# Giving out 48 late modulation blocks anew, and cutting the up projection's first parts into 18, 9 and 7 pairs

## The chip, the cores and the metric

The kernel runs on one core of a Trainium2 chip. The metric is the device time of one execution, in microseconds (us). Before the change three runs gave 1270.31, 1273.58 and 1273.60 us, a median of 1273.58 us. A further execution was recorded by the hardware profiler. Engines carry the names of the profile: PE is the matrix engine, DVE the vector engine, ACT the scalar engine, POOL the general engine, and SP the engine whose queue issues the loads.

## The reference

One decoder layer over 256 tokens of width 2048, in float32. A conditioning vector c gives six modulation vectors through `silu(c) @ w_ada + b_ada` (2048 by 6 x 2048): shift and gain of the mixer's norm, a gate g1, shift and gain of the ffn's norm, and a gate g2.

```python
h   = modulate(rms_norm(x, norm_mix), mix_shift, mix_gain)
x   = x + g1 * (concat(retention(h), rwkv7(h), moba(h)) @ w_out)   # all three from h @ w_in
h   = modulate(rms_norm(x, norm_ffn), ffn_shift, ffn_gain)
u,v = split(depthwise_conv3(h @ w_up))                             # 2 x 5632 columns
x   = x + g2 * ((silu(v) * u) @ w_down)
out = rms_norm(x, norm_final)
```

This is a sketch of it: the RWKV-7 branch ends with a norm over each head and a gate, and each row of the formula reads the modulation vectors that stand in it.

## The kernel before, in words

**Weights as one stream.** All activations are held with the features on the partitions, in 16 blocks of 128 features by 256 tokens. Each weight matrix is cut into 128 by 128 blocks, 3200 in all, in the order in which PE uses them (`weight_order`). One load brings 16 blocks (1 MB): 52 loads for the input projection ("in"), 16 for the output projection ("out"), 88 for "up" and 44 for "down". Half a load, 8 blocks, is called a chunk here: in has the chunks 0 to 103, out 104 to 135, up 136 to 311, down 312 to 399.

**Three matmuls for a block.** For precision each chunk is split in two halves by `convert_until`: ACT casts it (`hi`, L465), then DVE subtracts (`lo`, L466). PE then runs three matmuls for each block: hi by hi (L1226), hi by the low half of the activations (L1227), and lo by hi (L1228), so a chunk is 24 matmuls. `hi` and `lo` have three buffers each (`CONVB`), so the split of chunk c can only start when PE is through with chunk c-3, and without its `lo` PE stops within the first block of chunk c.

**Modulation blocks in the same stream.** The 96 rows of `w_ada` (1 MB each) are loaded in the same stream. DVE multiplies each by silu(c) and sums it in one instruction (L420, in `ada_block`), and one small instruction adds the bias (L428) or makes the gain of the norm of it (L422). `LATE_ADA` says how many of the 48 blocks of g1, ffn shift and ffn gain go to each part of the stream, spread evenly within it: first the tail of the input projection (19 loads, chunks 66 to 103), then four groups of five out loads (the last has one), then the first three parts of up.

**Raw tiles.** Loaded blocks lie in three raw tiles of 1 MB (`RAWB`), in which modulation blocks and early weights take turns. From chunk 116 on, weights are loaded as two halves into tiles of another pool (`LEAD` limits how many; L347 issues every load). SP issues loads in order, and a load waits there until its tile is free.

**Out.** In the out stage the RWKV branch is still being finished in short tasks between the chunks (`run_tasks`): a state's pieces sp (L921), sb (L976), u (L948), U (L953), the sums yps (L984), then a head norm whose root is found by Newton steps of small DVE rows (`rsqrt`, L240 to L245), the result yc (L1002), its transpose yt on PE (L1006), the mixing rows (L1011, L1013) and the split of them (`mxhi` L435, `mxlo` L436). The outputs of out are added to x with L1066, and at the start of out x comes by four loads, each behind a small copy that reads one element of g1 (L1055, `out_start`).

**Up.** `ffn_start` waits for the sum of squares of the last out tile (acc, L1080), takes the mean on PE (nps, L1084), finds the root by the same Newton steps (DVE) and spreads it on PE (rs, L390). The first four blocks of features (`EARLY` tiles, `ffn_early`) are worked before the root is known and scaled afterwards (L1120). Then DVE makes the normed activations, rows xn (L446) and hlo (L448), one pair for each block of features. `UP_BEGUN` says how many of the 44 pairs of up columns are begun with features 0 to 3, 0 to 7 and 0 to 11 only.

**What sets the order.** The order of the source is handed to a scheduler, which may move instructions on each engine; what stands in the program of an engine then runs from top to bottom.

Of the kernel before, what the change touches and what calls it, by code (L numbers as in the profile page):

```python
# [17 lines left out]
NF = 16  # L18
# [11 lines left out]

VISITS = (30, 20, 17)

UP_BEGUN = (22, 8, 4)


def spread(*lists):
# [5 lines left out]
def weight_order():  # L42
# [51 lines left out]
    n = 0  # L94
    for b in UP_BEGUN:
        pairs.append(list(range(n, n + b)))
# [62 lines left out]
ADA = {"mix_shift": 0, "mix_gain": 16, "g1": 32, "ffn_shift": 48, "ffn_gain": 64, "g2": 80}  # L159
RAWB, EXTRA, CONVB, AHEAD = 3, 2, 3, 2  # L160

LATE_ADA = (18, 3, 3, 2, 0, 7, 7, 8)

EARLY = 8

# [2 lines left out]

CONST_PAD, SMALL_PAD = 32, 16

LEAD = ((116, 0), (145, 8), (152, 6), (164, 4), (172, 3), (186, 1))


def trunk(tc, A):
    nc = tc.nc
    V, S, PE, G = nc.vector, nc.scalar, nc.tensor, nc.gpsimd
# [27 lines left out]
    def s4(name, dt=F32):  # L204
        return arena.tile([128, 4, T], dt, tag="s4", name=nm(name))
# [98 lines left out]
    parts += [(up[cut_up[g]:cut_up[g + 1]], 2) for g in range(3)]  # L304
    for n, (part, after) in zip(LATE_ADA, parts):
        n_part = len(part) - after
# [12 lines left out]
    def lead():  # L319

        c = len(chunks)
        return next((n for end, n in LEAD if c < end), 0)

# [88 lines left out]
    mod = {n: const.tile([128, NF], F32, name=f"mod_{n}") for n in ADA}  # L412
# [635 lines left out]
    def run_until(ready):  # L1048
        while not ready():
            run_tasks(1)  # L1050

    def out_start():
        for g in range(4):
            x = s4("x1")
            S.copy(x[:, 0, 0:1], mod["g1"][:, NF - 1:])  # L1055
            G.dma_start(x, A["xT"][:, 4 * g:4 * g + 4, :])
            x1.append(x)
        for g in (0, 2):
            run_until(lambda: g in finished)
# [132 lines left out]
    first_down = first_up + len(ORDER["up"]) // 8  # L1192
    hooks.setdefault(first_mix, []).append(lambda: new_stage(mixer, "mixer", bufs=1))
    hooks.setdefault(first_out, []).append(out_start)
    hooks.setdefault(first_out + WAITS[0], []).append(lambda: wait_for(3))
    hooks.setdefault(first_out + WAITS[1], []).append(lambda: wait_for(1))
# [117 lines left out]
```

## Time and profile before

| what | value |
|---|---|
| median of three runs | 1273.58 us |
| profiled execution, whole | 1276.42 us |
| its span (first to last instruction) | 1274.6 us |
| mean granted clock of PE | 0.987 of full |
| PE busy | 1227.2 us (96%) |
| DVE busy | 1030.1 us (81%) |
| ACT busy | 651.2 us (51%) |
| data moved | 320.58 MB, 252 GB/s mean |

Busy shares are averages over the whole span. A stage is read better by itself: where PE is busy for the whole of a stretch, only less work for PE would shorten it; where PE has gaps, the row on PE's waits names the engine that ended each. In a timeline row the first number is the start, the second the time until the result is there. The next row of the same engine often starts a little earlier than the sum of the two, so the distance between two starts is what an instruction costs its engine.

### The profile page before, as it was taken

To read this page: it belongs to the slowest core of one execution; us is meant where nothing else is said; L and a number is where in the kernel's file an instruction comes from. 1 tells how busy PE (TensorE), PEld (TensorE's weight loads), DVE (VectorE), ACT (ScalarE), POOL (GpSimd) and SP (SyncE) were. 2 spreads that over 40 slices of the span, in tenths; PEclk is the share of its full clock that TensorE was granted. 3 is DMA by queue.
4 is the path that set the end of the run, shared out by engine and by line. 5 is a ranking of instruction groups with operands and counts; after the bars stand their busy time and mean duration, and the time that the engine had idled before them with its cause. 6 is when DMAs were issued, how large, how long until landed. Compare 5 with 4: busy or idle time off the path is not lost.

```text
span 1274.6 us, 25479 instructions
## 1 busy us (share of the span) xinstructions
PE 1227.2 (96%) x10608; PEld 1205.3 (95%) x10608; DVE 1030.1 (81%) x1607; ACT 651.2 (51%) x1043; POOL 42.6 (3%) x41
## 2 busy tenths in 40 slices
PE   5899999999999999899999999999999999999995
PEld 4899999989998889899999999999999999999995
DVE  6988989989988589899887999899866766666444
ACT  4354443756434534566555666666555544444441
POOL 0000000000000000600000000000000000000000
PEclk7999999999999999999999999999999999999998
DMA  9899877876654569677984565565655677767551
GB/s 387 343 365 334 341 300 273 300 261 229 230 179 166 199 240 412 241 281 254 357 308 172 193 223 200 197 232 198 216 196 188 228 263 271 285 250 288 196 199 67
DMA packets 49940, 320.58 MB, mean 252 GB/s; under 512 B 5536, under 2 KB 6048, under 8 KB 15776
## 3 DMA queue, kind: packets, MB, share of 16 engines
q1 hardware_dynamic: 48528, 315.10, 67.5%
q0 software_dynamic: 1008, 3.67, 0.8%
q8 instruction: 83, 1.36, 0.4%
q14 instruction: 33, 0.27, 0.1%
q10 hardware_dynamic: 288, 0.17, 0.1%
HBM read 316.83 MB, written 2.10 MB: 250 GB/s over the span
## 4 chain that ended last, share of the span: by engine, by line
PE 83%; DVE 7%; issue 5%; ACT 2%; DMA 1%; POOL 1%; DVEq 0%; ACTq 0%; POOLq 0%
PE mm L1226 25%; PE mm L1227 24%; PE mm L1228 24%; DVE raw L420 3%; DVE lo L466 2%; ACT hi L465 1%; PE pair L1228 1%; PE xx L787 1%; PE pair L1227 1%; PE pair L1226 1%; POOL acc L1080 1%; DMA dec<-dec 1%; PE akv L800 1%; DMA x<-xT 1%; PE cb L406 0%
## 5 line engine op out<-in xcount | busy, mean ns | idle before, releaser
L466 DVE TENSOR_TENSOR lo<-raw,hi 128x1024 fp32r<-128x1024 f32 x400 | 489.1, 1225 | 164.5 <-ACT hi L465 161.5
L465 ACT CAST hi<-raw 128x1024 fp32r<-128x1024 f32 x400 | 419.0, 1049 | 387.3 <-PE mm L1227 335.1
L1226 PE MATMUL mm<-hhi,hi 128*128 128x256 f32 x2016 | 561.0, 278 | 0.5 <-DVE proj L501 0.5
L1228 PE MATMUL mm<-hhi,lo 128*128 128x256 f32 x2016 | 559.8, 278 | 1.1 <-DVE lo L466 1.1
L1227 PE MATMUL mm<-hlo,hi 128*128 128x256 f32 x2016 | 559.8, 278 | 0.0
L1228 PEld LDWEIGHTS mm<-hhi,lo 128*128 128x128 f32 x2016 | 378.9, 188 | 2.4 <-DVE lo L466 1.9
L1226 PEld LDWEIGHTS mm<-hhi,hi 128*128 128x128 f32 x2016 | 379.4, 188 | 1.4 <-DVE proj L501 0.7
L1227 PEld LDWEIGHTS mm<-hlo,hi 128*128 128x128 f32 x2016 | 378.9, 188 | 0.9 <-issue 0.2
L420 DVE SCALAR_TENSOR_TENSOR raw<-raw,cb 128x2048 f32<-128x2048 f32 x96 | 219.8, 2290 | 6.1 <-DMA raw<-w_ada 4.9
L1226 PE MATMUL mm<-ghi,hi 128*128 128x256 f32 x704 | 194.8, 277 | 0.0
L1227 PE MATMUL mm<-glo,hi 128*128 128x256 f32 x704 | 194.8, 277 | 0.0
L1228 PE MATMUL mm<-ghi,lo 128*128 128x256 f32 x704 | 194.8, 277 | 0.0
L1226 PEld LDWEIGHTS mm<-ghi,hi 128*128 128x128 f32 x704 | 132.2, 188 | 0.0
L1228 PEld LDWEIGHTS mm<-ghi,lo 128*128 128x128 f32 x704 | 132.2, 188 | 0.0
L1227 PEld LDWEIGHTS mm<-glo,hi 128*128 128x128 f32 x704 | 132.1, 188 | 0.0
L1226 PE MATMUL mm<-mxhi,hi 128*128 128x256 f32 x256 | 72.9, 285 | 2.4 <-DVE x L1066 2.4
L1227 PE MATMUL mm<-mxlo,hi 128*128 128x256 f32 x256 | 73.1, 286 | 0.0
L1228 PE MATMUL mm<-mxhi,lo 128*128 128x256 f32 x256 | 72.5, 283 | 0.0
L1080 POOL TENSOR_TENSOR acc<-acc,nsq 128x256 f32<-128x256 f32 x28 | 36.6, 1309 | 792.9 <-ACT nsq L1079 792.5
L1226 PEld LDWEIGHTS mm<-mxhi,hi 128*128 128x128 f32 x256 | 49.0, 191 | 3.4 <-DVE x L1066 2.6
L1226 PE MATMUL pair<-hhi,hi 128*128 128x256 f32 x160 | 45.1, 295 | 6.9 <-ACT hi L465 5.0
L1228 PEld LDWEIGHTS mm<-mxhi,lo 128*128 128x128 f32 x256 | 48.8, 191 | 1.4 <-DVE lo L466 0.7
(292 smaller groups left out, 1281.8 us busy)
## 6 DMA issues: line engine op xcount, KB each, us to landing
raw<-w_ada SPq DMA_DIRECT2D x96, 1024.0 KB, 5.1
raw<-w_up SPq DMA_DIRECT2D x67, 1024.0 KB, 4.8
raw<-w_in SPq DMA_DIRECT2D x52, 1024.0 KB, 6.1
raw<-w_down SPq DMA_DIRECT2D x44, 1024.0 KB, 4.9
raw<-w_up SPq DMA_DIRECT2D x42, 512.0 KB, 8.4
raw<-w_out SPq DMA_DIRECT2D x18, 512.0 KB, 9.9
raw<-w_out SPq DMA_DIRECT2D x7, 1024.0 KB, 4.8
x<-xT SPq DMA_DIRECT2D x4, 512.0 KB, 5.6
```

The source lines that it names most:

```text
L420: V.scalar_tensor_tensor(raw, raw, 1.0, cb, op0=OP.mult, op1=OP.mult, accum_out=m)
L465: S.copy(flat(hi), src)
L466: V.tensor_tensor(flat(lo), src, flat(hi).bitcast(F32), op=OP.subtract)
L787: return PE.matmul(pe[e][:, o:o + 128], (Bt, Kt)[i][pb, f, sl], (At, Rt)[n][pb, f, sl], start=True, stop=True)
L800: PE.matmul(ps[:, 128 * i + 64 * e:128 * i + 64 * e + 64], xv[:, e, 128 * i:128 * i + 128], vT[:, h, 64 * hd:64 * hd + 64], start=True, st ...
L1080: (V if t == NF - 1 else G).tensor_tensor(norm["acc"], norm["acc"], sq, op=OP.add)
L1226: PE.matmul(ps, whi[:, j], hi, start=first and not (two and t % 2), stop=False, skip_group_check=two)
L1227: PE.matmul(ps, whi[:, j], lo, start=False, stop=False, skip_group_check=two)
L1228: PE.matmul(ps, wlo[:, j], hi, start=False, stop=last, skip_group_check=two)
```

## The change

Three tables of numbers and one index are changed.

```diff
-UP_BEGUN = (22, 8, 4)
+UP_BEGUN = (18, 9, 7)
-LATE_ADA = (18, 3, 3, 2, 0, 7, 7, 8)
+LATE_ADA = (8, 7, 5, 4, 0, 8, 8, 8)
-LEAD = ((116, 0), (145, 8), (152, 6), (164, 4), (172, 3), (186, 1))
+LEAD = ((116, 0), (145, 8), (152, 6), (164, 4), (172, 3), (188, 1))
     def out_start():
         for g in range(4):
             x = s4("x1")
-            S.copy(x[:, 0, 0:1], mod["g1"][:, NF - 1:])
+            S.copy(x[:, 0, 0:1], mod["g1"][:, 7:8])
             G.dma_start(x, A["xT"][:, 4 * g:4 * g + 4, :])
```

Of the 48 late blocks, 8 instead of 18 are spread over the tail of the input projection, 16 instead of 8 over out, 24 instead of 22 over the first three parts of up. The small copy ahead of the loads of x now reads element 7 of g1, the last that the input projection's tail still makes. The first three parts of up, 34 pairs together in both, have 11, 8 and 6 loads before, with limits at chunks 158, 174 and 186, and end at chunks 154, 172 and 193 after.

The scheduler answers with another order on every engine. Three places are shown. The first is SP, the loads just ahead of the first out load that goes in halves (out load 7 of 16, chunks 118 and 119). Before:

```order
L347 DMA raw_5201<-w_out 128x2048
L347 DMA raw_5315<-w_out 128x2048
L347 DMA raw_5391<-w_ada 128x2048
L347 DMA raw_5449<-w_ada 128x2048
L347 DMA raw_5441<-w_out 128x1024
L347 DMA raw_5442<-w_out 128x1024
```

After:

```order
L347 DMA raw_5367<-w_out 128x2048
L347 DMA raw_5417<-w_ada 128x2048
L347 DMA raw_5451<-w_ada 128x2048
L347 DMA raw_5490<-w_ada 128x2048
L347 DMA raw_5523<-w_ada 128x2048
L347 DMA raw_5594<-w_ada 128x2048
L347 DMA raw_5661<-w_ada 128x2048
L347 DMA raw_5419<-w_out 128x1024
L347 DMA raw_5420<-w_out 128x1024
```

Two modulation loads stood ahead of that weight load, and now six stand there.

The second place is DVE at the same chunks. The first row is the `lo` of chunk 117, the last that of chunk 118. Before:

```order
L466 TENSOR_TENSOR lo_5511<-raw_5315,hi_5510 128x1024
L976 TENSOR_TENSOR sb_4905<-sp_5233,pcs_5262 64x4x64 x2
L422 SCALAR_TENSOR_TENSOR mod_ffn_gain<-mod_ffn_gain,bias_166,vec 128x1
L420 SCALAR_TENSOR_TENSOR raw_5449,mod_ffn_shift<-raw_5449,cb 128x2048
L953 TENSOR_TENSOR U<-u_5286,R_3478 32x512
L466 TENSOR_TENSOR lo_5566<-raw_5441,hi_5565 128x1024
```

After, the first twelve rows from the `lo` of chunk 117 on:

```order
L466 TENSOR_TENSOR lo_5487<-raw_5367,hi_5486 128x1024
L245 SCALAR_TENSOR_TENSOR rsy_5127<-rsa_5128,rsy_5127 128x8
L420 SCALAR_TENSOR_TENSOR raw_5417,mod_ffn_shift<-raw_5417,cb 128x2048
L243 SCALAR_TENSOR_TENSOR rsa_5128<-rsy_5127 128x8
L1066 SCALAR_TENSOR_TENSOR x_4710<-mm_5496,mod_g_162,x_4710 128x256
L244 TENSOR_TENSOR rsa_5128<-rsa_5128,var_5124 128x8
L428 TENSOR_TENSOR mod_ffn_shift<-mod_ffn_shift,vec 128x1
L420 SCALAR_TENSOR_TENSOR raw_5451,mod_ffn_gain<-raw_5451,cb 128x2048
L245 SCALAR_TENSOR_TENSOR rsy_5127<-rsa_5128,rsy_5127 128x8
L422 SCALAR_TENSOR_TENSOR mod_ffn_gain<-mod_ffn_gain,bias_166,vec 128x1
L1002 TENSOR_TENSOR yc_5088<-yc_5088,rsy_5127 128x512
L420 SCALAR_TENSOR_TENSOR raw_5490,mod_ffn_shift<-raw_5490,cb 128x2048
```

Then come four pairs of mixing rows (L1011, L1013), eight instructions, and after them, up to the `lo` of chunk 118:

```order
L953 TENSOR_TENSOR U<-u_5160,R_3458 32x512
L1066 SCALAR_TENSOR_TENSOR x_4710<-mm_5549,mod_g_162,x_4710 128x256
L436 TENSOR_TENSOR mxlo_5155<-mix_rwkv_4873,mxhi_5154 128x4x128
L428 TENSOR_TENSOR mod_ffn_shift<-mod_ffn_shift,vec 128x1
L420 SCALAR_TENSOR_TENSOR raw_5523,mod_ffn_gain<-raw_5523,cb 128x2048
L976 TENSOR_TENSOR sb_4870<-sp_5054,pcs_5166 64x4x64 x2
L422 SCALAR_TENSOR_TENSOR mod_ffn_gain<-mod_ffn_gain,bias_166,vec 128x1
L420 SCALAR_TENSOR_TENSOR raw_5594,mod_ffn_shift<-raw_5594,cb 128x2048
L953 TENSOR_TENSOR U<-u_5224,R_3458 32x512
L466 TENSOR_TENSOR lo_5534<-raw_5419,hi_5533 128x1024
```

Between two `lo` that stood one L420 apart, five L420 stand now, with the end of a head norm and its mixing rows.

The third place is DVE early in up, between the `lo` of chunk 143 and that of chunk 144. Before, from the `lo` of chunk 142 to that of chunk 144:

```order
L466 TENSOR_TENSOR lo_6477<-raw_5959,hi_6476 128x1024
L448 SCALAR_TENSOR_TENSOR hlo_6380<-xn_6424,mod_ffn_shift,hhi_6379 128x256
L448 SCALAR_TENSOR_TENSOR hlo_6380<-xn_6428,mod_ffn_shift,hhi_6379 128x256
L446 SCALAR_TENSOR_TENSOR xn_6466<-x_4743,mod_ffn_gain,rs_ffn 128x256
L446 SCALAR_TENSOR_TENSOR xn_6480<-x_4743,mod_ffn_gain,rs_ffn 128x256
L466 TENSOR_TENSOR lo_6516<-raw_5960,hi_6515 128x1024
L448 SCALAR_TENSOR_TENSOR hlo_6465<-xn_6466,mod_ffn_shift,hhi_6464 128x256
L448 SCALAR_TENSOR_TENSOR hlo_6465<-xn_6480,mod_ffn_shift,hhi_6464 128x256
L466 TENSOR_TENSOR lo_6558<-raw_6099,hi_6557 128x1024
```

After, twelve rows that begin three rows behind the `lo` of chunk 143; the row of L245 is the last Newton step of the ffn norm, which stood behind the `lo` of chunk 140 before:

```order
L420 SCALAR_TENSOR_TENSOR raw_6620,mod_ffn_gain<-raw_6620,cb 128x2048
L245 SCALAR_TENSOR_TENSOR rsy_6276<-rsa_6277,rsy_6276 128x2
L420 SCALAR_TENSOR_TENSOR raw_6705,mod_ffn_shift<-raw_6705,cb 128x2048
L446 SCALAR_TENSOR_TENSOR xn_6363<-x_4707,mod_ffn_gain,rs_ffn 128x256
L446 SCALAR_TENSOR_TENSOR xn_6379<-x_4704,mod_ffn_gain,rs_ffn 128x256
L1120 TENSOR_TENSOR up_6320<-up_6320,rs_ffn 128x1024
L448 SCALAR_TENSOR_TENSOR hlo_6362<-xn_6363,mod_ffn_shift,hhi_6361 128x256
L422 SCALAR_TENSOR_TENSOR mod_ffn_gain<-mod_ffn_gain,bias_166,vec 128x1
L446 SCALAR_TENSOR_TENSOR xn_6383<-x_4704,mod_ffn_gain,rs_ffn 128x256
L428 TENSOR_TENSOR mod_ffn_shift<-mod_ffn_shift,vec 128x1
L420 SCALAR_TENSOR_TENSOR raw_6778,mod_ffn_gain<-raw_6778,cb 128x2048
L420 SCALAR_TENSOR_TENSOR raw_6790,mod_ffn_shift<-raw_6790,cb 128x2048
```

Ten more rows follow (four L448, four L446, one L1120, one L422) before the `lo` of chunk 144. Where two L448 stood between the two `lo`, four L420, seven L446, five L448 and two L1120 stand now.

## Rows read from the trace of the kernel before

**Rows 1.** Stretches: start:end, length; PE, PEld, DVE, ACT, POOL busy (count), PEclk, DMA, GB/s.
```profile
203.90:441.00 237.10, 228.17 (x1874) 212.87 (x1873) 209.73 (x444) 127.89 (x277) 5.75 (x9) 0.99 0.63 227
418.20:421.60 3.40, 3.40 (x15) 3.04 (x14) 1.16 (x1) 1.33 (x3) 0.00 (x0) 0.50 0.92 316
541.50:561.90 20.40, 20.34 (x169) 20.16 (x169) 20.11 (x38) 13.53 (x39) 0.00 (x0) 1.00 0.76 287
600.00:700.00 100.00, 100.00 (x885) 100.00 (x884) 81.40 (x104) 53.97 (x79) 0.00 (x0) 1.00 0.78 281
```

**Rows 2.** PE's waits from 203.9 us on: total us, times, longest us.
```profile
PE mo_pt L605 <- ACT mo_p L602: 2.7, 2, 2.3
...
PE y L874 <- DVE bd L864: 1.4, 1, 1.4
```

**Rows 3.** Timeline of DVE in out: start, us, engine, line, operation.
```profile
456.84 0.69 DVE L1002 TENSOR_TENSOR yc<-yc,rsy 128x512 f32<-128x512 f32 x1
457.44 2.28 DVE L420 SCALAR_TENSOR_TENSOR raw<-raw,cb 128x2048 f32<-128x2048 f32 x1
...
459.65 0.60 DVE L1011 SCALAR_TENSOR_TENSOR mix_rwkv<-yt,vec,rwm 128x128 f32<-128x128 f32 x2
...
461.74 0.67 DVE L953 TENSOR_TENSOR U<-u,R 32x512 f32<-32x512 f32 x1
462.34 1.20 DVE L466 TENSOR_TENSOR lo<-raw,hi 128x1024 fp32r<-128x1024 f32 x1
463.48 0.67 DVE L436 TENSOR_TENSOR mxlo<-mix_rwkv,mxhi 128x512 fp32r<-128x512 f32 x1
464.08 0.86 DVE L976 TENSOR_TENSOR sb<-sp,pcs 64x256 f32<-64x256 f32 x2
464.97 0.48 DVE L1066 SCALAR_TENSOR_TENSOR x<-mm,mod_g,x 128x256 f32<-128x256 f32 x1
465.37 1.22 DVE L466 TENSOR_TENSOR lo<-raw,hi 128x1024 fp32r<-128x1024 f32 x1
```

**Rows 4.** The same timeline, the `lo` of chunks 117 and 118.
```profile
467.74 1.22 DVE L466 TENSOR_TENSOR lo<-raw,hi 128x1024 fp32r<-128x1024 f32 x1
...
472.93 1.23 DVE L466 TENSOR_TENSOR lo<-raw,hi 128x1024 fp32r<-128x1024 f32 x1
```

**Rows 5.** Pieces of the chain that ended last, in out: start, us, what.
```profile
457.58 0.66 PE yt L1006 x4
458.24 0.99 PE u L948 x8
...
463.19 0.62 PE sp L921 x32
```

**Rows 6.** Timeline of ACT in out.
```profile
420.27 0.37 ACT L435 CAST mxhi<-mo_o 128x256 fp32r<-128x256 f32 x1 [0.59 <-PE mo_o L615]
...
496.40 1.05 ACT L465 CAST hi<-raw 128x1024 fp32r<-128x1024 f32 x1 [2.46 <-PE mm L1227]
497.36 0.62 ACT L435 CAST mxhi<-mix_rwkv 128x512 fp32r<-128x512 f32 x1
```

**Rows 7.** Timeline of DVE, 421 to 423 us; in brackets idle time before, and releaser.
```profile
421.98 0.48 DVE L1066 SCALAR_TENSOR_TENSOR x<-mm,mod_g,x 128x256 f32<-128x256 f32 x1 [2.62 <-DMA x<-xT]
422.38 0.41 DVE L436 TENSOR_TENSOR mxlo<-mo_o,mxhi 128x256 fp32r<-128x256 f32 x1
```

**Rows 8.** Timeline of DVE at the start of up.
```profile
540.24 0.43 DVE L1080 TENSOR_TENSOR acc<-acc,nsq 128x256 f32<-128x256 f32 x1 [1.45 <-POOL acc L1080]
...
547.70 0.16 DVE L245 SCALAR_TENSOR_TENSOR rsy<-rsa,rsy 128x2 f32<-128x2 f32 x1
...
549.14 0.88 DVE L446 SCALAR_TENSOR_TENSOR xn<-x,mod_ffn_gain,rs_ffn 128x256 f32<-128x256 f32 x2
549.94 1.22 DVE L1120 TENSOR_TENSOR up<-up,rs_ffn 128x1024 f32<-128x1024 f32 x1
551.07 0.87 DVE L448 SCALAR_TENSOR_TENSOR hlo<-xn,mod_ffn_shift,hhi 128x256 fp32r<-128x256 f32 x2
```

## The prediction

> **What bounds the kernel now.** I read the busy shares by stretch first. PE is busy for the whole of the up projection (100.00 of 100 us in 600 to 700, 885 matmuls, so 113 ns for one and 24 x 0.113 = 2.71 us for a chunk), and also where up begins, 20.34 of 20.4 us [rows 1]. There DVE works 20.11 of the same 20.4 us: both engines are full, and the `lo` of each chunk comes just before PE wants it. In the stretch from 203.9 to 441 us, which holds most of the input projection and the start of out, PE is idle 237.10 - 228.17 = 8.9 us, while DVE is busy 209.73 us of it [rows 1]. The list of PE's waits says that these gaps are small and many. The longest single one, 2.3 us, is for ACT's mo_p, another of 1.4 us for DVE's bd [rows 2]. [...] All that the change can give back on the input side is therefore 8.9 + 1.7 = 10.6 us. What it can cost has no such bound: wherever DVE falls behind PE, PE stops.
>
> **The change part by part.** I go by the order of the engines' programs after the change, and by durations from the trace before. The distance between the starts of two rows is what an instruction costs its engine.
>
> (a) *Ten modulation blocks fewer in the input projection's tail.* One L420 costs 459.65 - 457.44 = 2.21 us [rows 3], so DVE has 22 us less to do there. That stretch has 8.9 us of PE idle time, and what ended the two long waits is attention and RWKV work on ACT and DVE that only indirectly waits for L420. Bounds: 0 and -10.6 us. I take the middle, -5, about the 2.3 us wait with its clock and a part of the small ones.
>
> (b) *Eight blocks more in out.* They don't fall evenly. Between the `lo` of chunk 117 and that of chunk 118 stood one L420, and the two `lo` started 472.93 - 467.74 = 5.2 us apart [rows 4]. Now five L420 stand there, with the end of a head norm and its mixing rows. The DVE work in between, from distances in the timeline of out [rows 3]: five L420 11.05; yc 457.44 - 456.84 = 0.60; the eight mixing rows 461.74 - 459.65 = 2.09; two U at 0.60; two L1066 at 0.40; mxlo 0.60; the two sb 0.89; eight small rows, at some 0.15 each as an estimate, 1.2. Sum 18.4 us.
>
> What PE can do meanwhile is bounded by the buffers. The split of chunk 117 can't start before PE is through with chunk 114. Counted from then, ACT's cast takes 1.05 us [rows 6], the `lo` of 117 then 463.48 - 462.34 = 1.14 us [rows 3], the 18.4 us follow, and the `lo` of 118 takes 1.14 more: 21.7 us. PE has until then chunks 115, 116 and 117, 3 x 2.71 = 8.1 us, and of RWKV one yt (0.66), three pieces of u with the yps beside them (0.99 each) and two of sp (0.62 each) [rows 5]: 13.0 us. The difference is 8.7 us at the least. Some of the rows wait for PE, ACT or a load, so I take +10. SP speaks for the upper side: six modulation loads stand ahead of the weights of chunk 118 where two stood, the sixth must wait for a raw tile that only the third L420 of this list frees, and the weights land behind it. I give this up to 4 us more, no more than two L420's time. Bounds +8.7 and +14.
>
> One row decides whether these L420 can be stepped over: DVE waited 2.62 us for a load of x, and the mxlo behind it, whose other input ACT had finished at 420.27 + 0.37 = 420.64, started at 422.38, after that x [rows 6, 7]. So DVE takes its rows in turn, a ready row too. [...] By it the term stands; could the `lo` overtake, the term would be nothing. [...]
>
> (c) *The second transpose of RWKV's result.* On PE, yt stood 0.12 chunks into chunk 122 and now stands 0.08 into chunk 124, while the first matmul that needs its product stays at 124.5. After yt (0.66 [rows 5]) come the eight mixing rows 2.09, then the casts: ACT's mxhi, 0.62 [rows 6], lies beside one `lo` of 1.14, and the mxlo takes 0.67 to its end [rows 3]. That is 0.66 + 2.09 + 1.14 + 0.67 = 4.6 us from the start of yt, and PE has in this time yt itself and 0.42 x 2.71 = 1.1 us. PE waits 2.8, say +3 us. Before, 2.4 chunks, 6.5 us, covered it. Lower bound 0 (if DVE has caught up enough to split without that `lo` and yc comes early), upper 5.
>
> (d) *Start of up.* Before, the root of the ffn norm was ready 547.86 - 540.67 = 7.2 us after acc [rows 8]. In the new order, between acc and the last Newton row (L245), DVE has five L420 (11.05), five `lo` (5.7), and some 17 small rows at 0.15 as an estimate (2.6): 19.3 us. The spreading of the root on PE (rs) was moved back by the scheduler to 4.4 chunks behind nps, which PE reaches 4.4 x 2.71 = 11.9 us after acc. PE waits 7 us there. Then, between that L245 and the `lo` of chunk 144, stand three L420 (6.63), seven L446 at 0.40, five L448 at the same (durations 0.88 and 0.87 for two), two L1120 at 551.07 - 549.94 = 1.13 [rows 8], small rows 0.4, and the `lo` itself 1.14: 15.2 us. PE has from 141.5 to 144 2.5 chunks, 6.8 us, and rs, about 0.5 us as an estimate. It waits some 7.5 us again. Both together +14. Since the same L420 hold both, a floor comes from the buffers: the `lo` of 143 starts 1.05 us after PE starts chunk 141 at the earliest, and with 1.14, some 2.7 (one L420 and small rows), 14.1 and 1.14 the `lo` of 144 ends 20.1 us after it; PE has 3 chunks, 8.1, and 0.5: 11.5 us. Upper bound 18, should the loads of the eight blocks that stand in this stretch come late as well.
>
> (e) *Clock.* Waits of 7 us and more are longer than the one of 2.3 us after which 3.40 us ran at half clock; the packed stretches further on run at full clock again [rows 1, 2]. There are three or four such waits (chunk 118, rs, 144, perhaps yt). At 1.7 us each I take three, +5. Bounds 0 and 7.
>
> (f) *Parts of 18, 9 and 7 pairs, `LEAD`, element 7 of g1.* The pairs begun are 34 as before, and so are the matmuls and the partial evacuations. Features 4 to 7 are wanted from chunk 154 instead of 158; DVE starts their rows some 8 chunks earlier, and PE is held up before by (d), which gives DVE time. The two new blocks in the up parts are 2 x 2.21 us in a stretch where DVE is busy 81.40 of 100 us [rows 1], so hidden by PE's work; without that cover they would cost 4.4. The small copy still reads the last g1 block that the tail makes. Value 0, bounds -2 and +4.
>
> Sum: -5 + 10 + 3 + 14 + 5 + 0 = +27 us. The profiled execution took 1276.42 us (span 1274.6 and 1.8 around it), so it would take 1303.4; it is 2.84 us above the median of the runs, so the median comes to 1300.6. I say 1300.
>
> **Rivals.** *Only one of the two bunches decides.* If PE, held at 118, lets DVE run so far ahead that the rows of up come earlier, or if at 118 PE arrives later than I think, either (b) or (d) with its clock falls away: about 13 us less, 1287. For it: what stops PE once gives DVE slack. Against it: three buffers limit how far `lo` can run ahead, and by these the floors 8.7 and 11.5 were worked out separately.
>
> *Loads come late as well.* SP's six loads ahead of the out weights, and eleven in a row early in up, hold weights behind raw tiles that DVE frees. With the upper ends of (b) to (e), and -5 for (a), +14 + 5 + 18 + 7 + 4 - 5 = +43, 1316. For it: SP is in order, and the raw tiles are three. Against: up's weights have tiles of their own.
>
> *Relief wins (the other side).* The tail of the input projection gives back all 10.6 us, as its DVE is busy 209.73 of 237.10 us, and the bunches of L420 are met by a PE that is late anyway, so that they cost nothing: 1276.42 - 10.6 - 2.84 = 1263. It decides from the point where the waits at chunks 118, 124 and 144 with rs together are below 10.6 us. Against it: the floor of (d) alone is 11.5.
>
> *An even trade.* Waits of about 10 us in all against the full relief: 1274.
>
> **How the numbers follow.** Forecast as above 0.70; only one bunch 0.13; late loads 0.07; relief wins 0.06; even trade 0.04. Bounds for the range: the low end takes (b) and (d) at their floors with no clock loss, no wait at yt and full relief, 8.7 + 11.5 - 10.6 = +9.6, 1283; the high end +42, 1316. It leaves out the last two cases and tails. This kernel's measurement tells apart about 0.3%, 4 us. Slower by more: 0.70 + 0.13 + 0.07 = 0.90. Faster by more: 0.06. Within: 0.04.
>
> **What would show it.** In the profile after: PE waiting about 10 us for the `lo` of chunk 118, with five L420 in a row of DVE's work ahead of it; a wait of rs for L245 and one for the `lo` of chunk 144 of some 7 us each; stretches of 3.4 us at clock 0.5 behind them; one wait for mxlo near chunk 124; the idle time of PE up to chunk 104 smaller by about half; up from chunk 150 on packed as before. It is wrong if PE has no wait above 3 us between chunks 115 and 145, or if these waits are there and the total is not longer, which would mean that the input tail gave back more than the trace lets it have.

## The result and the profile after

The changed kernel took 1302.80, 1308.11, 1308.43 and 1320.94 us, a median of 1308.27 us against 1273.59 us before (now of four executions): a ratio of 1.0289, 95% interval 1.0258 to 1.0320. It is slower by about 35 us. Of several kernels below some executions take 15 to 25 us more than the others; the ratios leave most of these out, and the medians given with the runs are over all executions. The profiled execution is the fastest of the four (1302.80 us), and it is the one to hold against the sum of the prediction, which was made for the profiled execution and came to 1303.4 us.

The busy times of the whole span, after:

```profile
span 1301.0 us, 25483 instructions
PE 1233.3 (95%) x10608; PEld 1210.3 (93%) x10608; DVE 1029.9 (79%) x1607; ACT 652.1 (50%) x1043; POOL 42.3 (3%) x41
```

The span grew by 26.4 us. PE has the same 10608 matmuls and is busy for 1233.3 us instead of 1227.2: 6.1 us more for the same work, of which (e) below tells more. The other 20.3 us are idle time of PE. DVE has no more work than before (1029.9 us against 1030.1). The list of PE's waits from 203.9 us on (total us, times, longest us) says what ended them:

```profile
PE rs L390 <- DVE rsy L245: 7.8, 2, 5.4
PE mm L1226 <- ACT silu_c L1135: 4.7, 1, 4.7
PE mm L1228 <- DVE lo L466: 3.7, 3, 2.2
PE u L948 <- DVE sb L976: 3.6, 2, 3.4
PE mm L1226 <- DVE x L1066: 3.1, 2, 2.7
PE sp L921 <- DVE U L953: 2.7, 1, 2.7
PE y L874 <- DVE bd L864: 2.6, 1, 2.6
PE mo_pt L605 <- ACT mo_p L602: 2.5, 2, 1.8
```

The two last were there before [rows 2]. New among those of 2.5 us and more are four in two places: sp and u, between the matmuls of chunks 117 and 118, and rs and the wait for silu_c (L1135) at chunk 141.5. The stretches (start:end, length; PE, PEld, DVE, ACT, POOL busy; PEclk, DMA, GB/s) of the input stage with the start of out, of chunk 118, and of the start of up with a part of it:

```profile
203.90:441.00 237.10, 229.46 (x1882) 215.86 (x1880) 195.50 (x421) 127.85 (x276) 5.71 (x9) 0.98 0.54 192
421.80:432.00 10.20, 10.20 (x84) 9.29 (x83) 5.28 (x7) 2.70 (x6) 0.00 (x0) 0.50 0.76 270
473.00:486.60 13.60, 9.25 (x88) 7.73 (x83) 10.89 (x15) 5.69 (x11) 0.00 (x0) 0.50 1.01 362
547.00:604.00 57.00, 43.35 (x342) 42.14 (x341) 52.78 (x82) 26.91 (x69) 2.90 (x3) 0.91 0.85 329
568.60:578.60 10.00, 4.58 (x19) 4.29 (x20) 10.00 (x15) 3.12 (x12) 0.00 (x0) 0.50 0.94 341
```

Before, beside the half-clock stretch of [rows 1], there was one at the end of out:

```profile
527.40:530.90 3.50, 3.50 (x16) 3.50 (x17) 2.41 (x5) 1.58 (x3) 2.21 (x2) 0.51 0.57 239
```

The first row answers to the first of [rows 1]: DVE is busy 195.50 us there instead of 209.73, and still PE is idle 7.6 us where it was 8.9. The second, third and fifth rows are half-clock stretches of 10.2, 13.6 and 10.0 us. The first of them stands where before one of 3.40 us stood, the other two are new, and the one at the end of out came again, with 3.4 us.

On DVE the rows between the `lo` of chunks 117 and 118 (timeline: start, us, operation) answer to [rows 4]:

```profile
460.23 1.23 DVE L466 TENSOR_TENSOR lo<-raw,hi 128x1024 fp32r<-128x1024 f32 x1
...
461.45 2.29 DVE L420 SCALAR_TENSOR_TENSOR raw<-raw,cb 128x2048 f32<-128x2048 f32 x1
...
464.28 2.28 DVE L420 SCALAR_TENSOR_TENSOR raw<-raw,cb 128x2048 f32<-128x2048 f32 x1
...
467.35 2.28 DVE L420 SCALAR_TENSOR_TENSOR raw<-raw,cb 128x2048 f32<-128x2048 f32 x1
...
471.64 0.67 DVE L953 TENSOR_TENSOR U<-u,R 32x512 f32<-32x512 f32 x1
...
473.30 2.27 DVE L420 SCALAR_TENSOR_TENSOR raw<-raw,cb 128x2048 f32<-128x2048 f32 x1
...
475.51 0.85 DVE L976 TENSOR_TENSOR sb<-sp,pcs 64x256 f32<-64x256 f32 x2
...
476.52 2.28 DVE L420 SCALAR_TENSOR_TENSOR raw<-raw,cb 128x2048 f32<-128x2048 f32 x1
...
479.56 2.36 DVE L466 TENSOR_TENSOR lo<-raw,hi 128x1024 fp32r<-128x1024 f32 x2
```

The two `lo` start 19.3 us apart instead of 5.2; the prediction's sum was 18.4 and the `lo` itself 1.14. DVE never rests in between, and U and sb, for which PE waits 2.7 and 3.4 us, stand in this one line: PE goes on with sp at 472.37 and with u at 476.41 us, 0.06 and 0.05 us after DVE is through with them.

The weights of chunk 118 come late as well. The first two lines are SP's loads (start, us from the first to the last of a group), the third one of ACT's waits from 455 to 500 us:

```profile
455.24 14.75 SPq L347 DMA_DIRECT2D raw<-w_ada  x6
470.09 23.92 SPq L347 DMA_DIRECT2D raw<-w_out  x14
```

```profile
ACT hi L465 <- DMA raw<-w_out: 0.9, 3, 0.6
```

The sixth modulation load goes out at 469.67 us, just after the third of the five rows has ended (469.64), and the weights go out behind it, from 470.09 us on. ACT stands 0.56 us for them and casts `hi` of chunk 118 at 478.23 us; PE, through with u, waits 1.0 us for this `hi`. Before, that `hi` was cast at 471.33 us, 10 us before PE began the chunk. So at chunk 118 two paths end close together, the rows on DVE and the weights, and the weights are late because the same rows hold the raw tiles of the loads ahead of them.

At the start of up, in answer to [rows 8]:

```profile
550.10 0.43 DVE L1080 TENSOR_TENSOR acc<-acc,nsq 128x256 f32<-128x256 f32 x1 [1.44 <-POOL acc L1080]
...
569.11 0.15 DVE L245 SCALAR_TENSOR_TENSOR rsy<-rsa,rsy 128x2 f32<-128x2 f32 x1
...
583.17 1.22 DVE L466 TENSOR_TENSOR lo<-raw,hi 128x1024 fp32r<-128x1024 f32 x1
```

From the end of acc to the end of the root it is 569.26 - 550.53 = 18.7 us (the prediction had 19.3; before, 7.2), and from there to the end of the `lo` of chunk 144 15.1 us (15.2). And three rows of ACT tell why PE waits for silu_c:

```profile
570.58 0.37 ACT L400 COPY rs_ffn<-rs 128x256 f32<-128x256 f32 x1 [7.13 <-PE rs L390]
...
574.36 0.51 ACT L447 ACTIVATE hhi<-xn,mod_ffn_shift 128x256 fp32r<-128x256 f32 x1 [1.55 <-DVE xn L446]
...
575.03 0.16 ACT L1135 COPY silu_c<-mm 128x1 f32<-128x1 f32 x1
```

ACT stands 7.13 us before the copy of the spread root, then again for DVE's xn, and the copies of PE's results (L1133, L1135) stand behind both on ACT, from 574.78 us on. So PE, whose next weight matmul waits 4.7 us for silu_c in the list above, stops a second time. No `hi` of the chunks 136 to 151 waits for a load: here the weights are not late.

### The profile page after: what moved, and what is told of

Its sections match the earlier page's. It is cut to its first block, busy times and chain, and to the rows that moved or that the text cites. A ratio compares the mean times of both kernels' runs of the same rounds, so it can differ in the third digit from the quotient of the medians.

```text
span 1301.0 us, 25483 instructions
## 1 busy us (share of the span) xinstructions
PE 1233.3 (95%) x10608; PEld 1210.3 (93%) x10608; DVE 1029.9 (79%) x1607; ACT 652.1 (50%) x1043; POOL 42.3 (3%) x41
## 4 chain that ended last, share of the span: by engine, by line
PE 80%; DVE 11%; DMA 4%; ACT 2%; issue 2%; POOL 1%; DVEq 0%; ACTq 0%; SPq 0%; POOLq 0%
PE mm L1226 24%; PE mm L1228 23%; PE mm L1227 23%; DVE raw L420 4%; DVE lo L466 3%; DMA raw<-w_up 1%; ACT hi L465 1%; DMA raw<-w_out 1%; PE pair L1228 1%; PE pair L1226 1%; PE pair L1227 1%; PE xx L787 1%; DMA raw<-w_ada 1%; POOL acc L1080 1%; PE akv L800 1%
## 5 line engine op out<-in xcount | busy, mean ns | idle before, releaser
L420 DVE SCALAR_TENSOR_TENSOR raw<-raw,cb 128x2048 f32<-128x2048 f32 x96 | 219.5, 2287 | 9.6 <-DMA raw<-w_ada 8.5
L1226 PE MATMUL mm<-mxhi,hi 128*128 128x256 f32 x256 | 76.6, 300 | 4.3 <-DVE x L1066 3.1
L1227 PEld LDWEIGHTS mm<-mxlo,hi 128*128 128x128 f32 x256 | 51.2, 200 | 0.6 <-issue 0.5
```

The costliest lines, as they stand in the source:

```text
L420: V.scalar_tensor_tensor(raw, raw, 1.0, cb, op0=OP.mult, op1=OP.mult, accum_out=m)
L1226: PE.matmul(ps, whi[:, j], hi, start=first and not (two and t % 2), stop=False, skip_group_check=two)
L1227: PE.matmul(ps, whi[:, j], lo, start=False, stop=False, skip_group_check=two)
```

## The experiments

The theory (A) was that modulation rows, put together on DVE, hold the rows that PE waits for. Its rivals were: all of the loss comes from giving out the blocks (B), or from the new parts (C); DVE has too much to do, wherever the rows stand (D); weights land late behind more modulation loads (E). F and G come with the runs that they belong to.

To compare stages, this table has the time that PE takes from its first matmul of one chunk to that of another, as a difference to before, from the profiled execution of each kernel (us, to about 0.1, worked out from the starts of the matmuls in the traces). Chunks 60 to 112 are the input projection's end with the start of out, 112 to 138 are most of out, 138 to 150 the start of up.

| kernel | ratio to before (95%) | 60-112 | 112-138 | 138-150 | 150-399 |
|---|---|---|---|---|---|
| changed kernel | 1.0289 (1.0258-1.0320) | -1.7 | +13.8 | +15.5 | +1.1 |
| late_only | 1.0143 (1.0105-1.0181) | -3.6 | +11.2 | +8.7 | +1.0 |
| parts_only | 1.0155 (1.0119-1.0190) | +0.8 | +1.2 | +14.1 | +6.3 |
| after_tied | 1.0146 (1.0109-1.0182) | -7.6 | +17.7 | +7.3 | +24.9 |
| before_tied | 1.0132 (1.0079-1.0185) | +2.7 | -0.6 | +1.0 | +13.2 |
| parts_root | 1.0118 (1.0051-1.0185) | +0.6 | -3.7 | +7.9 | +20.9 |
| after_root | 1.0105 (1.0067-1.0143) | -3.8 | +8.5 | +3.5 | +6.1 |
| late13 | 1.0069 (1.0044-1.0094) | -1.3 | +7.4 | +0.8 | +3.1 |
| after_chain | 1.0199 (1.0177-1.0222) | -5.1 | +17.7 | +3.6 | +6.7 |
| after_thin | 0.9957 (0.9926-0.9988) | -5.3 | -4.1 | +1.2 | +3.2 |
| before_thin | 0.9917 (0.9899-0.9934) | -5.3 | -2.4 | +0.4 | 0.0 |
| before_root | 0.9992 (0.9978-1.0005) | +0.7 | -5.0 | +0.7 | +1.5 |
| t20_root | 1.0214 (1.0194-1.0234) | +4.6 | -4.3 | +0.6 | +26.1 |

Three things limit what a column says. The profiled execution of the kernel before is 2.84 us above the median of its runs, so that the columns of a row can together be some 3 us too low. The chunks up to 60, which no edit concerns, are left out; there the kernels took 0 to 5 us less than before. And at the same granted clock PE starts a matmul every 113 ns or every 118 ns (885 or 851 in 100 us at clock 1.00, rows in the last section), and often stays with one for long. In the last column an execution that falls into the slower spacing loses up to 26 us; the profiles of after_tied, parts_root and t20_root did so early. In the first three stages the number of matmuls at the slower spacing differs from kernel to kernel as well (718 after and 552 before in chunks 60 to 112), which at 4.5 ns each is at most 2 us of a column.

**late_only: the blocks given out anew, the parts as before.**

```diff
-LATE_ADA = (18, 3, 3, 2, 0, 7, 7, 8)
+LATE_ADA = (8, 7, 5, 4, 0, 8, 8, 8)
-            S.copy(x[:, 0, 0:1], mod["g1"][:, NF - 1:])
+            S.copy(x[:, 0, 0:1], mod["g1"][:, 7:8])
```

> The kernel before with the new giving-out of the 48 blocks and the copy that reads element 7, but with the old parts (22, 8, 4). DVE's order still has the five modulation rows between the lo of chunks 117 and 118; between those of 143 and 144 it has one, not four. Theory A (bunched modulation rows on DVE hold PE): the out bunch costs as after, some 12 us with its clock; the root of the ffn norm still stands behind three of them, some 5 us: about 1290 us, between before and after. Rival B (all of the loss comes from giving the blocks out later, the parts cost nothing, as the prediction's point f had it): as after, 1303 to 1308. Rival C (the loss comes from the parts): as before, 1274.

Median 1294.76 us, 5 us above what A expected, and neither B nor C. PE's waits in this kernel:

```profile
PE u L948 <- DVE sb L976: 3.6, 2, 3.4
PE mm L1226 <- ACT silu_c L1135: 3.3, 1, 3.3
...
PE sp L921 <- DVE U L953: 2.7, 1, 2.7
PE rs L390 <- DVE rsy L245: 2.2, 1, 2.2
```

At chunk 118 the waits for U and sb are those of the changed kernel to the tenth of a microsecond. At the start of up, with three modulation rows ahead of the root, rs waits 2.2 us and the matmul behind silu_c 3.3.

**parts_only: the parts, with nothing else.**

```diff
-UP_BEGUN = (22, 8, 4)
+UP_BEGUN = (18, 9, 7)
-LEAD = ((116, 0), (145, 8), (152, 6), (164, 4), (172, 3), (186, 1))
+LEAD = ((116, 0), (145, 8), (152, 6), (164, 4), (172, 3), (188, 1))
```

> The kernel before with the parts (18, 9, 7) and the changed lead, the 48 blocks given out as before. DVE's order has one modulation row between the lo of chunks 117 and 118, as before, but four between those of 143 and 144, and four ahead of the root of the ffn norm. Theory A: no wait at 118; waits at rs and near chunk 144 with a half-clock stretch, some 15 us: about 1289. Rival B (the parts cost nothing): 1274. Rival C (the loss comes from the parts alone): 1303 to 1308.

Median 1295.36 us: not B, and between A (1289) and C (1303). Out takes 1.2 us more, and the start of up loses 14.1 us, as in the changed kernel, with the same two waits (from 400 to 640 us):

```profile
PE mm L1226 <- ACT silu_c L1135: 7.2, 2, 4.7
PE rs L390 <- DVE rsy L245: 4.1, 1, 4.1
```

The limit in LEAD was changed together with the parts and not by itself. So the parts, which were thought to cost nothing, make the bunch early in up: the first part has 9 loads instead of 11, its seven or eight modulation blocks are spread over these less the last two, and more of them come ahead of the root. Either edit brings a loss there (8.7 and 14.1 us), and both together are paid about once (15.5 us).

**after_thin and before_thin: modulation rows over 256 of 2048 columns.**

```diff
-        V.scalar_tensor_tensor(raw, raw, 1.0, cb, op0=OP.mult, op1=OP.mult, accum_out=m)
+        n = 256 if p in ("g1", "ffn_shift", "ffn_gain") else 2048
+        V.scalar_tensor_tensor(raw[:, 0:n], raw[:, 0:n], 1.0, cb[:, 0:n], op0=OP.mult, op1=OP.mult, accum_out=m)
```

> The changed kernel, in which the 48 late modulation blocks are multiplied and summed over the first 256 of their 2048 columns only, so that most of DVE's work on them is left out; every load stays. DVE has 14 us less in out and 15 us less early in up. Theory A (DVE's time on these rows): 1262 to 1276. Rival E (the weights land late behind more modulation loads): above 1295.

> Control for the changed kernel with short modulation rows: the kernel before, in which the 48 late blocks are summed over 256 of 2048 columns and the rest is left out. If with short rows the giving-out and the parts no longer matter, it takes what that kernel took, 1265 to 1270; if the change still costs by its loads or parts, it is more than 5 us faster than that one.

Medians 1267.93 and 1262.62 us. These two kernels leave out seven eighths of the sum of these rows, so they do not compute the layer. The loss of the change is gone: in the two bad stages the changed kernel takes -4.1 and +1.2 us, the kernel before -2.4 and +0.4. Between the two 5.3 us are left. In the profiles 3.2 us of difference lie behind chunk 150, where 21 chunks of the first ran at the slower spacing, and 2.7 before chunk 60, where no edit acts; in out and at the start of up together the change costs nothing.

But more than DVE's time is changed here. The scheduler answers to the shorter rows with another order: in after_thin no more than two of them stand between two `lo`, one instead of five stands ahead of the root, and SP no longer issues six modulation loads in a row. So the loss hangs on the time of these rows and on the order that is made of it, and E is not excluded by this run: with the bunch the late weights are gone too. What can be said of E comes from the traces. In the changed kernel PE waits 1.0 us for weights at chunk 118. In after_root, with the same five rows and the same six loads, the weights are there in time, and PE waits 2.7 us for U and 2.9 for sb all the same. Had only U and sb come early in the changed kernel, the late weights would have held PE to about the same time.

**after_root, parts_root, before_root: the root of the ffn norm first.** The same rule for the changed kernel, for parts_only and for the kernel before: the source's later modulation rows may not be issued ahead of the last Newton step.

```diff
+    newton, root = [None], [None]
...
-            V.scalar_tensor_tensor(y, a, 1.5, y, op0=OP.add, op1=OP.mult)
+            newton[0] = V.scalar_tensor_tensor(y, a, 1.5, y, op0=OP.add, op1=OP.mult)
...
-                ada_block(it[1], it[2], raw[0])
+                with tc.issue_after(root[0]) if root[0] is not None and len(chunks) < 150 else nullcontext():
+                    ada_block(it[1], it[2], raw[0])
...
+        root[0] = getattr(newton[0], "ins", newton[0])
```

The last line stands in `ffn_start`, where `newton[0]` is the last Newton step of this norm.

> The changed kernel with the rule that keeps modulation rows behind the root of the ffn norm. The bunch of five at chunk 117 stays, the one at 143 and the wait for the root are gone. Theory A: only the loss in out stays, so as the run with the late blocks alone less its 8 us early in up: 1282 to 1290. If both bunches overlapped in what they cost, 1300 or more.

> The kernel before with the parts (18, 9, 7) and one rule for DVE's order: the modulation rows that come after the last Newton step of the ffn norm in the source, up to chunk 150, may not be issued ahead of it. The blocks, their loads and the parts are those of the run with the parts alone (1295). In DVE's order no modulation row is left ahead of the root and no more than one stands between two lo. Theory A (the rows ahead of the root and the bunch behind it are what the parts cost): 1272 to 1279. Rival F (the shorter parts cost by themselves, by evacuations, wanted features or loads): 1290 to 1297.

> Control for the rule: the kernel before with no modulation row ahead of the root of the ffn norm. Before, one row stood there and PE did not wait for the root, so theory A expects 1270 to 1276. If the rule itself costs several us, what the two kernels with the rule show is to be read against it.

Medians 1289.43, 1298.02 and 1273.82 us. On the changed kernel the rule takes the start of up from +15.5 to +3.5 us, as A expected, and what stays is out (+8.5) and 6.1 us behind it. On the parts alone the time lies a little above what F had, and far from A. But most of the 22 us of its profile stand behind chunk 150, where the profiled execution (1298.56 us) ran at the slower spacing from chunk 222 on; the six executions lie far apart (1278.53 to 1304.35 us), and of the others no trace exists. At the start of up the rule takes the loss from +14.1 to +7.9, not to nothing; a wait of 2.9 us for ACT's copy of up is left there, so part of what F supposed may be true. On the kernel before the rule changes the total by nothing that can be measured.

**late13: thirteen and thirteen.**

```diff
-LATE_ADA = (18, 3, 3, 2, 0, 7, 7, 8)
+LATE_ADA = (13, 5, 4, 4, 0, 7, 7, 8)
-            S.copy(x[:, 0, 0:1], mod["g1"][:, NF - 1:])
+            S.copy(x[:, 0, 0:1], mod["g1"][:, 12:13])
```

> The kernel before with 13 late blocks in the input projection's tail, 13 in out and 22 in up (13, 5, 4, 4, 0, 7, 7, 8), the copy reading element 12, the parts as before. DVE's order has no more than two modulation rows between two lo, and the first transpose of RWKV's result stands at chunk 113.4 as before. Theory A (the bunch of five): 1272 to 1280. Rival D (each block more in out costs, about 20 us for eight): about 1287.

Seven of the twelve executions took 1282.38 to 1285.74 us, the other five 1303.58 to 1306.34; the ratio of 1.0069 lies between what A and D expected. There is no bunch of five, and still out loses 7.4 us, at another place, RWKV's second transpose (timeline of DVE):

```profile
496.26 0.16 DVE L245 SCALAR_TENSOR_TENSOR rsy<-rsa,rsy 128x8 f32<-128x8 f32 x1
...
496.40 2.28 DVE L420 SCALAR_TENSOR_TENSOR raw<-raw,cb 128x2048 f32<-128x2048 f32 x1
...
498.61 0.68 DVE L1002 TENSOR_TENSOR yc<-yc,rsy 128x512 f32<-128x512 f32 x1
...
502.20 2.28 DVE L420 SCALAR_TENSOR_TENSOR raw<-raw,cb 128x2048 f32<-128x2048 f32 x1
...
504.41 0.68 DVE L436 TENSOR_TENSOR mxlo<-mix_rwkv,mxhi 128x512 fp32r<-128x512 f32 x1
```

One modulation row stands between the root and yc, one between the mixing rows and mxlo. PE waits 1.1 us for yt, which reads yc, 2.9 us for ACT's mxhi, which needs the mixing rows, and 1.1 us for mxlo. Here single rows of 2.28 us, with no bunch, stand in DVE's chain at a place where PE waits for what the chain makes, 5.1 us in these three waits.

**after_tied and before_tied: modulation rows kept at their place between the `lo`.**

```diff
-                ada_block(it[1], it[2], raw[0])
+                with tied(pos[0]):
+                    ada_block(it[1], it[2], raw[0])
...
```

The helper `tied`, not shown, is `issue_after` the `lo` of the half load before the row.

> The changed kernel with one more rule for the order of DVE: each modulation row may be issued only behind the lo of the half load that stands before it in the stream, so that no more than two stand between two lo anywhere. The same blocks are given out in the same parts. Theory A: no long wait at chunk 118 or 144, about as before, 1270 to 1280. Rival D (DVE has too much to do in out and early in up, wherever the rows stand): as after, above 1295. Rival E (the weights land late behind more modulation loads): as after or little better, above 1290.

> The kernel before with the same rule for DVE's order. Before has no two modulation rows between two lo from chunk 66 on, so theory A expects little: 1268 to 1278. If the rule itself costs or gains (the rows of RWKV move with it), it shows here and is to be taken off the result of the changed kernel with the rule.

Medians 1294.57 and 1293.12 us. The rule alone costs the kernel before some 17 us, most of it behind chunk 150, where PE waits for ACT's `hi` (4.7 us in four waits) and two half-clock stretches of 3.4 us stand. Both expectations of theory A failed. Under the rule the change costs 1.5 us by the medians, but this proves little: in the table, whose row for after_tied is from its slowest execution (1318.34 us), the changed kernel still loses 17.7 us in out, spread over more places (waits of 1.7 us for U, 1.5 for sb, 2.9 for mxhi, 4.3 for x), and wins elsewhere. A alone, as bunches, falls for out: spreading sixteen blocks does not help.

**after_chain: the RWKV chain first.**

```diff
-                ada_block(it[1], it[2], raw[0])
+                with tc.issue_after(getattr(newton[0], "ins", newton[0])) if 104 <= len(chunks) < 150 else nullcontext():
+                    ada_block(it[1], it[2], raw[0])
...
```

> The changed kernel with one rule for DVE's order from chunk 104 to 150: a modulation row that comes behind a Newton chain in the source (RWKV's two head norms, the ffn norm) may not be issued ahead of its last step. As many blocks as in the changed kernel are worked in out, 16, with the same loads. RWKV's first transpose goes back from chunk 117.9 to 113.5; three modulation rows instead of five stand in the fullest place. Theory G (in out the rows hold the RWKV chain, and with it PE, not the number of blocks alone): 1272 to 1281. Rival D (the number of blocks in out costs): as the changed kernel with the rule for the ffn root alone, 1285 to 1290.

Median 1298.61 us, worse than the rule for the ffn root alone and outside what G and D expected. PE's waits from 200 us on:

```profile
PE yt L1010 <- DVE mod_g L431: 7.6, 1, 7.6
PE mm L1232 <- DVE lo L470: 7.4, 8, 1.7
PE mm L1230 <- ACT hi L469: 6.6, 3, 4.8
```

The first transpose yt now comes at chunk 113.5, without a long wait. But the second moved forward as well, from chunk 124.1 in the changed kernel to 116.0, is reached long before DVE has made its input yc, and holds PE for 7.6 us. Three modulation rows held back by the rule stand one each ahead of yc, of the mixing rows and of mxlo, and ACT's `hi` stands behind mxhi, which needs these mixing rows: PE waits another 4.8 us. With sixteen blocks in out the loss went to another place each time it was pushed. Whether any order of sixteen blocks would fit there (against D) stays open.

**t20_root: the other direction, as a version to beat both.** With it goes the rule for the root.

```diff
-LATE_ADA = (18, 3, 3, 2, 0, 7, 7, 8)
+LATE_ADA = (20, 2, 2, 2, 0, 7, 7, 8)
...
```

> The other direction, as a version that may beat both: 20 late blocks in the input projection's tail, 6 in out, 22 in up (20, 2, 2, 2, 0, 7, 7, 8), with the rule for the root of the ffn norm; the copy reads the last element of g1. Theory A and D: DVE has 4 us less in out, so 1265 to 1274. If the input projection's tail is limited by these rows, as the changed kernel supposes, 1274 to 1282.

All four executions took 1298.77 to 1301.14 us. By chunk 150 the kernel is 0.9 us behind before, counted from chunk 60. The rest is the spacing of PE's matmuls: this row of its packed stretch

```profile
700.00:800.00 100.00, 100.00 (x851) 100.00 (x850) 88.90 (x154) 61.28 (x93) 0.00 (x0) 1.00 0.59 200
```

has 851 matmuls in 100 us where before had 885 [rows 1], at clock 1.00. So it neither beats before nor tells what two blocks fewer in out are worth. Of the ten kernels here that compute the whole layer none is faster than the kernel before.

## Why the prediction was right, and where a step was not

The direction, the time and the kind of cause came out as forecast: 1300 forecast, 1308 measured, and 1303.4 against 1302.8 for the profiled executions. The last is luck in part, since terms that were off cancelled: the relief came 3 us short, out cost some 2.6 us less than 10 + 3 with the clock of two waits, and 2.2 us were won before chunk 60, where the change does nothing.

(a) The relief of the input projection was put at -5; measured, -1.7 us from chunk 60 to 112. Idle time fell from 8.9 to 7.6 us, but the half-clock stretch near 422 us lasted 10.2 us instead of 3.4, so by half of the 6.8 us more, as an estimate, 3.4 us of the relief went back. No run shows by itself the 1.7 us that the bound of 10.6 and (e) have for the clock: it is half of the 3.40 us at clock 0.50 in [rows 1]. What the traces of before and after show is that in the half-clock stretches most of the weight matmuls that follow one another start 213 or 214 ns apart, and at clock 1.00 mostly 113 or 118 ns. The sign that PE's idle time up to chunk 104 would be half did not come: from chunk 60 on it was 4.8 us, 4.2 before. Most of the 22 us that DVE no longer works there were on no path to PE.

(b), (c) Out was put at 10 + 3 with some clock; measured, +13.8 us with its clock. The five rows on DVE took what the sum said (19.3 us). That PE would wait at the `lo` of 118 was not quite it: the same line of DVE rows also held U and sb, which PE asked for first (2.7 and 3.4 us), and the `lo` was ready 1.5 us after PE had begun the chunk, while PE worked at another piece of sp. So this `lo`, whose `hi` ended only at 479.27 us, does not show whether a ready row could have stepped over the L420; that DVE takes its rows in turn is shown by the one row of [rows 6, 7], a start at 422.38 us with inputs ready at 420.64, and the rows from the `lo` of 117 to that of 118 (460.23 to 479.56 us) started in the order of its program. The late weights, given up to 4 us, held PE for 1.0. The second transpose cost less than 3: from chunk 122 to 127 the changed kernel fell back by 1.0 us, with waits of 0.3 us for yc and 0.2 for mxhi and none for mxlo.

(d) The start of up was put at 14 and clock; measured, +15.5 us with clock. rs waited 5.4 us (7 forecast): DVE took 18.7 us, and PE came to rs 13.4 us after acc and not 11.9, since the chunks 138 to 140, with matmuls 258 columns wide, took 2.87 us each (119 ns from start to start) and not 2.71. The 7.5 us at chunk 144 came as 4.7 us at chunk 141.5, because ACT's copies, for which PE waited, stood behind the root and behind xn, which the prediction had not seen, and 2.2 us for a `lo` at chunk 146.

(e) Clock was put at 5, as three stretches of 3.4 us; it was more. From 204 us to the end of up there were two half-clock stretches of 3.4 us before, and four after, of 10.2, 13.6, 3.4 and 10.2 us. PE worked 27.8 us in them instead of 6.8; half of the difference, some 10.5 us as an estimate from the share of 0.50, is what the clock cost. PE's busy time over the whole span grew by 6.1 us only, in the main because 758 fewer of the matmuls up to chunk 60 ran at the spacing of 118 ns, which at 4.5 ns is 3.4 us.

(f) This step failed: the parts were put at 0. Alone they cost 1.55%, in the main by the bunch of (d), which the prediction read correctly from the order without asking which edit had made it. Since the order of the changed kernel as a whole was read, the total did not suffer; a reader who had kept the parts and dropped the new giving-out would have lost some 20 us.

The rival of late loads, as something that comes on top, was worth 1.0 us at chunk 118 and nothing at the start of up; as a second path behind the same rows it is not excluded for out. That the relief wins was refuted by the size of (d). The even trade and the single bunch did not come: both bunches cost. That the median of the runs lies 5.5 us above the profiled execution was not forecast; 18 us of the slowest run would fit a part of it at the slower spacing, but no trace of that run exists.

What is shown and what is not: at the start of up, holding the rows back behind the root takes most of the loss away while the same rule changes nothing on the kernel before. In out the rows are traced as what PE waits behind, but no run put the same sixteen blocks there without a loss, save the one that cut the rows short and changed the order with it.

## What to carry to other kernels

Numbers that move independent work are to be judged by the order that comes out of the scheduler: list what now stands ahead of each row that the critical engine waits for, add up durations from the trace, and compare with what that engine has left to do within its buffers. Vary each number alone as well, since an edit that looks free (the parts here) can be what makes the other's bunch. DVE, 81% busy before, had room on average and none at the places where its chain was the critical one; there single rows of 2.28 us stood ahead of what PE waited 1.1, 2.9 and 1.1 us for (late13).

## What the runs showed of the hardware that was not expected

At a granted clock of 1.00, PE starts its matmuls 113 ns apart in some stretches and 118 ns in others, in the same program. In parts_only:

```profile
600.00:680.00 80.00, 80.00 (x709) 80.00 (x708) 55.46 (x62) 41.92 (x66) 0.00 (x0) 1.00 0.64 228
690.00:790.00 100.00, 100.00 (x851) 100.00 (x850) 79.35 (x128) 58.41 (x86) 0.00 (x0) 1.00 0.56 194
800.00:900.00 100.00, 100.00 (x885) 100.00 (x884) 94.09 (x169) 65.79 (x101) 0.00 (x0) 1.00 0.61 208
```

The change to 118 ns came at chunk 184.25, right behind a wait of PE for a `lo` of 1.3 us, and the change back at chunk 222.25, behind one of 0.4 us. In t20_root it began at chunk 154.25, behind 0.2 us, and lasted to the end. But the changed kernel waited 0.7 us at chunk 222 and stayed at 113 ns, and after_thin changed at chunk 201 without a wait, behind one matmul that started 135 ns after the one before it. The order of PE's program does not decide either: up to chunk 60 it is the same in the kernel before and in the changed one, and 1219 and 461 of 1440 matmuls there came at the slower spacing. So the same packed stretch, with PE busy for the whole of it (100.00 of 100 us in the last two rows), took 4% more or less time: not only less work for PE can shorten such a stretch, and nothing in these traces tells why. What sets the spacing was not tried and stays open.

In the changed kernel the half-clock stretches are not set by the length of the wait ahead of them alone: after the 1.8 us wait for mo_p at 418 us 10.2 us ran at half clock, around the waits of 2.7 and 3.4 us at chunk 118 it was 13.6 us, and behind the waits of 2.6 us at 382 us and 2.2 us at 591 us none did. The one at chunk 118 has many small RWKV matmuls and waits among them, 88 matmuls in 13.6 us.
